# Low parts of all split weight tiles subtracted on VectorE, none on GpSimd

## The chip, the cores and the metric

The kernel runs on one core of one Trainium2 chip. The metric is the device time of one execution in microseconds (us). PE is TensorE, DVE is VectorE, ACT is ScalarE, POOL is GpSimd, SP the engine from whose queue the weights are loaded. Times inside the program are counted from the start of the profiled span.

## The reference

Two stacked blocks on 256 tokens of width 1024, all in float32. The first mixes a gated delta rule (8 heads) with a dilated window attention and ends in a mixture of 64 experts; the second prepends 16 meta tokens and runs an attention layer and a short-convolution layer, each followed by a squared-ReLU layer. Cut to what matters here:

```python
def first_block(x, c, w_ada, ..., w_in, ...):
    cs = jax.nn.silu(c)
    mod = (cs @ w_ada[l] + b_ada[l])[:, None, :]
    h = _rms(x, g_mix[l]) * (1.0 + sc1) + sh1
    proj = h @ w_in[l]                       # 1024 x 11280
    y_a = gated_deltanet(gq, gk, gv, gz, gb, ga, ...)
    y_b = dilated_mixture(dil_q, dil_k, dil_v, ...)
    merged = sigmoid(gate_a) * (y_a @ w_up_gdn[l]) + sigmoid(gate_b) * (y_b @ w_up_dil[l])
    x = x + gt1 * (merged @ w_out[l])
    x = x + gt2 * moe_ffn(h2, ...)

def second_block(x, meta_tokens, norm_g, w_in, w_out, ..., w_up, w_down):
    for i in range(2):
        h = _rmsnorm(hres, norm_g[i, 0])
        m = _diff_attention(h, ...) if i == 0 else _short_conv(h, ...)
        hres = hres + _rmsnorm(m, norm_g[i, 1])
        h = _rmsnorm(hres, norm_g[i, 2])
        hres = hres + _rmsnorm(_sqrelu_mlp(h, w_up[i], w_down[i]), norm_g[i, 3])
```

## The kernel before

Every dense product outside the experts is made of three products of float32r tiles, so that nearly all bits of float32 are kept: weights and activations are each split into a high part and a low part, and `mm3` (L168 to L175) adds high by high (L172), high by low (L173) and low by high (L175). A weight tile of 1024 x 256 comes from HBM through a ring of four buffers (`load`). `split` (L148 to L159) makes the two parts of half of it, 128 partitions by 1024 numbers: ACT copies the high part `hi` (L154), then one engine subtracts it from the weights to get the low part `lo` (L158). That engine is POOL for some of the tiles and DVE for the rest. The tiles `hi` and `lo` rotate through three buffers each in the first stage and through four in the second block. PE needs `hi` first and `lo` for the last third of the product.

Two counters choose the engine. `pool_every = 4` holds while the delta rule, the dilated attention and the gates are computed (from 42 to 452 us, called the delta-rule stage below): there every fourth split goes to POOL, 21 in all. `pool_next = 2` is set ahead of four layers of the second block (attention, first squared-ReLU layer, convolution, second squared-ReLU layer) and sends the next two splits to POOL, 8 in all. One small tile more (`gbl`, L563) is subtracted on POOL once. Besides, POOL computes all powers of -1/2 (`rpow` L236, `token_factors` L1533, L667) and some small scalings.

A scheduling layer sets the order of the instructions on each engine from its own estimates, within the data's order. Each engine then works through its own list in that order; an instruction that waits holds back what stands behind it on its engine.

The end of a layer in the second block is one chain. `mix_out` (L1677 to L1694) makes the last eight products `m` on short tiles (256 numbers), adds their squares into `accm` (ACT squares `sq`, DVE adds at L1516), and `add_normed` then sums over the partitions on PE (L1529), reduces (`tp`, L1531), takes the power on POOL (`tr`, L1533), spreads it on PE (L1540), and updates the residual on DVE (L1587, L1588), from which ACT and DVE make the next layer's activations `hsh` and `hsl`. Three groups of ten matmuls that fill time (`warm`, L1572) stand between. The next layer begins with `wide` (L208), three tiles side by side. The second squared-ReLU layer follows `mix_out` in the same way with 256 tokens for 258. The end of the first squared-ReLU layer, ahead of the convolution, has the same chain behind a plain product.

Of the kernel before, what the change touches and what calls it, by code (L numbers as in the profile page):

```python
# [10 lines left out]
F32 = mybir.dt.float32  # L11
# [3 lines left out]
ALU = mybir.AluOpType  # L15
# [107 lines left out]
class Kern:  # L123
    def __init__(self, ctx, tc, a, out, dbg=None, stop=None):
        self.ctx, self.tc, self.nc, self.a, self.out = ctx, tc, tc.nc, a, out
        self.dbg = dbg or {}
        self.stop = stop
        self.ns, self.pool_every, self.pool_next = 0, 0, 0
        self.steps, self.queued = [], []
        E = ctx.enter_context  # L130
        self.cst = E(tc.tile_pool(name="cst", bufs=1))
        self.ring = E(tc.tile_pool(name="ring", bufs=4))
# [15 lines left out]
    def split(self, v, hp, shape=None):  # L148

        nc = self.nc  # L150
        a, b = v.shape[1], v.shape[2]
        hi = hp.tile([128, 1024], F32R, tag="hi", name="hi")[:, :a * b].rearrange("p (a b) -> p a b", a=a)
        lo = hp.tile([128, 1024], F32R, tag="lo", name="lo")[:, :a * b].rearrange("p (a b) -> p a b", a=a)
        nc.scalar.activation(hi, v, AF.Copy)  # L154
        self.ns += 1
        eng = nc.gpsimd if self.pool_next > 0 or self.pool_every and self.ns % self.pool_every == 0 else nc.vector
        self.pool_next -= 1
        eng.tensor_tensor(lo, v, hi.bitcast(F32), op=ALU.subtract)  # L158
        return hi, lo  # L159

    def wcols(self, w, col, n=256):
# [193 lines left out]
    def phase_a(self):  # L355
        nc, tc, a, cst = self.nc, self.tc, self.a, self.cst
        with ExitStack() as st:
# [31 lines left out]
            with tc.manual_schedule():  # L389
# [55 lines left out]
                v = self.load(self.wcols(w_in, OFF_GK), (8, 256))  # L445
# [13 lines left out]
            with tc.tile_pool(name="wka", bufs=1) as wk:  # L459
                self.second_setup(xt.tile([16, D], F32, name="mt", tag="thb"),  # L460
                                  wk.tile([128, 4, 64], F32, name="lv", tag="cv", bufs=2),
                                  wk.tile([128, 2, 64], F32, name="lvp", tag="cth", bufs=2),
                                  pm.tile([128, 512], F32, tag="m", name="ps_mt"))
                late = (y for c in (2, 4, 3, 5) for u in range(2) for y in self.ada(c, u))
                self.pool_every = 4
                self.fill = lambda: next(late, None)
                dil = [self.dil_pair(n, w_in, x, hp, wk) for n in range(2)]
                for pr in range(4):
                    t = self.gdn_proj(pr, w_in, x, hp, wk)
                    if pr == 0:  # L470
                        nc.sync.dma_start(self.CA, a["consts"][:, C_LVL:C_ND])
                        to_channels(x_tok, xT)
                    self.gdn_pair(pr, t, wk)
                    for n in (0, 0, 0, 0, 1)[pr:pr + 1] if pr < 2 else ((0, 0), (1,))[pr - 2]:
                        next(dil[n])
                list(dil[1])
                th = (xt.tile([128, 8, T], F32, name="tha", tag="xnT"), xt.tile([128, 8, T], F32, name="thb", tag="thb"))
                for u in range(4):
                    for n, off in enumerate((OFF_GA, OFF_GBT)):
                        def sink_g(ft, ps, n=n, u=u):  # L480
                            nc.scalar.activation(th[n][:, u * 2 + ft, :], ps, AF.Tanh, scale=0.5)
                        self.dense(self.wcols(w_in, off + u * 256), x, T, sink_g, hp, pp)
                        self.fill()
                list(late)
            self.dump("yaT", ya)
            self.dump("ybT", yb)
            self.pool_every = 0
            sh.close()
            self.before_b()
            hp = sh.enter_context(tc.tile_pool(name="hpf", bufs=3, side="right"))  # L490
# [65 lines left out]
    def gdn_scalars(self, w_in, x, hp, wk):  # L556

        nc, a, cst, pm = self.nc, self.a, self.cst, self.pm
        small = self.small
        v = self.load(w_in[:, OFF_GB:OFF_GB + 16].rearrange("(j p) c -> p j c", p=128), (8, 16))  # L560
        hi, lo = (wk.tile([128, 8, 16], F32R, tag=t, name=n) for t, n in (("dv0", "gbh"), ("dv1", "gbl")))
        nc.scalar.activation(hi, v, AF.Copy)
        nc.gpsimd.tensor_tensor(lo, v, hi.bitcast(F32), op=ALU.subtract)  # L563
        xh, xl = x
        gb = cst.tile([128, 2, 16], F32, name="gb")
        ps = pm.tile([128, 512], F32, tag="m", name="ps_gb")
        self.mm3(ps[:16, :T], lambda j: hi[:, j, :], lambda j: lo[:, j, :], lambda j: xh[:, j, :], lambda j: xl[:, j, :], 8)
        gbt = wk.tile([16, T], F32, name="gbt", tag="cv", bufs=2)
        nc.vector.tensor_copy(gbt, ps[:16, :T])
        ps = pm.tile([128, 512], F32, tag="m", name="ps_gbt")  # L570
        for t in range(2):
            nc.tensor.transpose(ps[:, t * 16:t * 16 + 16], gbt[:, t * 128:t * 128 + 128], self.ident[:16, :16])
        nc.vector.tensor_copy(gb, ps[:, :32].rearrange("p (t c) -> p t c", t=2))
        self.beta = cst.tile([128, 2, 8], F32, name="beta")
        nc.scalar.activation(self.beta, gb[:, :, 0:8], AF.Tanh, scale=0.5)
        nc.vector.tensor_scalar(self.beta, self.beta, 0.5, 0.5, op0=ALU.mult, op1=ALU.add)
        al = cst.tile([128, 2, 8], F32, name="alog")
        nc.scalar.dma_start(al[:, 0, :], pbc(a["gdn_a_log"][0]))
        nc.scalar.dma_start(al[:, 1, :], pbc(a["gdn_dt_bias"][0]))
        nc.scalar.activation(al[:, 0, :], al[:, 0, :], AF.Exp)  # L580
        z = small.tile([128, 2, 8], F32, tag="z", name="z")
        for t in range(2):
            nc.vector.tensor_tensor(z[:, t, :], gb[:, t, 8:16], al[:, 1, :], op=ALU.add)

        u = small.tile([128, 2, 8], F32, tag="u", name="u")
        nc.vector.scalar_tensor_tensor(u, z, -1.0, z, op0=ALU.mult, op1=ALU.min)
        nc.scalar.activation(u, u, AF.Exp)
        s = small.tile([128, 2, 8], F32, tag="s", name="s")
        nc.vector.tensor_scalar(s, u, 2.0, None, op0=ALU.add)
        nc.vector.reciprocal(s, s)  # L590
        nc.vector.tensor_tensor(s, s, u, op=ALU.mult)
        s2 = small.tile([128, 2, 8], F32, tag="s2", name="s2")
        nc.vector.tensor_tensor(s2, s, s, op=ALU.mult)
        q = small.tile([128, 2, 8], F32, tag="q", name="q")
        nc.vector.tensor_scalar(q, s2, 2.0 / 17, None, op0=ALU.mult)
        for k in (15, 13, 11, 9, 7, 5, 3):
            nc.vector.scalar_tensor_tensor(q, q, 2.0 / k, s2, op0=ALU.add, op1=ALU.mult)
        nc.vector.scalar_tensor_tensor(q, q, 2.0, s, op0=ALU.add, op1=ALU.mult)
        nc.vector.scalar_tensor_tensor(q, z, 0.0, q, op0=ALU.max, op1=ALU.add)
        self.g = cst.tile([128, 2, 8], F32, name="g")  # L600
        for t in range(2):
            nc.vector.scalar_tensor_tensor(self.g[:, t, :], q[:, t, :], -1.0, al[:, 0, :], op0=ALU.mult, op1=ALU.mult)

        ps = pm.tile([128, 512], F32, tag="m", name="ps_gc")
        gf = self.g.rearrange("p a b -> p (a b)")
        nc.tensor.matmul(ps[:, 0:16], self.ut, gf, start=True, stop=True)
        nc.tensor.matmul(ps[:, 16:24], self.lt, self.g[:, 0, :], start=True, stop=True)
        self.ngc = cst.tile([128, 3, 8], F32, name="ngc")
        nc.vector.tensor_scalar(self.ngc[:, 0:2, :].rearrange("p a b -> p (a b)"), ps[:, 0:16], -1.0, None, op0=ALU.mult)
        nc.vector.tensor_copy(self.ngc[:, 2, :], ps[:, 16:24])  # L610
        self.dump("beta", self.beta)
        self.dump("g", self.g)
# [978 lines left out]
    def phase_c(self):  # L1591
        nc, tc, a, cst = self.nc, self.tc, self.a, self.cst
        with ExitStack() as st:
# [7 lines left out]
            with tc.tile_pool(name="ppa", bufs=3, space=PSUM) as self.pp, \  # L1601
# [5 lines left out]
                b = None  # L1607
                bank = lambda: self.pt.tile([128, 512], F32, tag="t", name="ps_row")
                oT = xp.tile([128, 8, 258], F32R, name="oh", tag="oh"), xp.tile([128, 8, 258], F32R, name="ol", tag="ol")
                self.pool_next = 2  # L1610
                qkv, b = self.diff_proj(0, h, lambda: self.token_factors(acc, 272, bank), ap, hp,
                                        lambda r: self.kept(self.rows_of(*r, 272, bank), 272, sp))
                for pr in range(4):
# [12 lines left out]
            h, acc = self.gained(4, 258, xp, self.upd)  # L1626
            yT = xp.tile([128, 8, 258], F32R, name="oh", tag="oh"), xp.tile([128, 8, 258], F32R, name="ol", tag="ol")
            w = a["w_in_2"][1]
            self.pool_next = 2
            with tc.tile_pool(name="cvp", bufs=2) as ap:  # L1630
                for u in range(4):
                    c2, y = [None] * 2, [None] * 2
# [64 lines left out]
    def mlp(self, layer, n, hp, sp, xp, bank):  # L1697
# [1 line left out]

        nc, a, pp = self.nc, self.a, self.pp  # L1700
        h, acc0 = self.gained(layer * 4 + 2, n, xp, self.upd)
        self.pool_next = 2
        m = None if layer else xp.tile([128, 8, 258], F32, name="m", tag="m")
        wu, wd = a["w_up_2"][layer], a["w_down_2"][layer]
        acc, add = self.token_sums(sp, n, "q")
# [344 lines left out]
```

## Time and profile before

| what | value |
|---|---|
| median of 3 runs | 1692.33 us (1687.98 to 1697.52) |
| the profiled execution's own time | 1685.4 us |
| its span, first to last instruction | 1683.3 us |
| granted TensorE clock, mean over the span | 0.983 |
| PE / DVE / ACT / POOL busy | 95% / 57% / 40% / 8% |

A clock share of 1.00 is 2.4 GHz, 0.50 is 1.2 GHz. The busy share of PE is one of modelled ends of pipelined matmuls, so small waits do not show in it. In the views, "idle before" and the name in brackets tell what an engine waited for; `x8` at a row's end counts merged instructions, and their time is that from the first one's start to the last one's end. The durations of neighbours on one engine overlap a little, so that a step in the list costs somewhat less than its duration.

### The profile page before, as it was taken

The numbers are of one execution on the slowest core, as the hardware profiler recorded it, in microseconds if no ns is written. First come the engines' busy times: TensorE is split into PE (matmuls) and PEld (weight loads), VectorE is DVE, ScalarE is ACT, GpSimd is POOL, SyncE is SP. The second block draws the span as 40 slices with busy tenths as digits, with TensorE's granted clock in tenths as the row PEclk, the third lists the DMA queues.
The fourth block names the chain that finished last, engine by engine and source line by source line (L and its number), as shares of the span: only waits on it lengthen the run. The fifth ranks groups of instructions, "written<-read, shape, count | busy, mean of one in ns | idle before, by whom it ended". The sixth has DMA issues, their size and how long they took to land. (4 is left out here: it accounts for less than half of the span.)

```text
span 1683.3 us, 31624 instructions
## 1 busy us (share of the span) xinstructions
PE 1604.9 (95%) x12847; PEld 1406.0 (84%) x12847; DVE 960.0 (57%) x2069; ACT 676.1 (40%) x1353; POOL 135.9 (8%) x120
## 2 busy tenths in 40 slices
PE   6999999999999999998999997998999999989998
PEld 3899999999997667655766656888999999989998
DVE  5879796975475223322332345666765457686644
ACT  4534335344453212211221214555554345465532
POOL 0211212132100000000000001012000010010000
PEclk8999999999999999999999998999999999989999
DMA  9534442456389799999999995322555545455552
GB/s 315 200 127 150 136 140 91 161 182 189 123 275 381 303 420 418 420 418 419 420 368 409 419 412 166 109 88 88 176 176 183 190 154 165 148 161 184 183 177 75
DMA packets 198496, 392.04 MB, mean 233 GB/s; under 512 B 8760, under 2 KB 158780, under 8 KB 173260
## 3 DMA queue, kind: packets, MB, share of 16 engines
q1 hardware_dynamic: 197916, 389.76, 63.7%
q8 instruction: 102, 1.67, 0.4%
q14 instruction: 46, 0.38, 0.1%
q10 hardware_dynamic: 432, 0.23, 0.1%
HBM read 388.92 MB, written 1.05 MB: 232 GB/s over the span
## 5 line engine op out<-in xcount | busy, mean ns | idle before, releaser
L154 ACT ACTIVATE hi<-w 128x1024 fp32r<-128x1024 f32 (+3 forms) x316 | 314.8, 1003 | 345.2 <-PE proj L173 231.2
L158 DVE TENSOR_TENSOR lo<-w,hi 128x1024 fp32r<-128x1024 f32 (+3 forms) x287 | 330.6, 1156 | 175.1 <-ACT hi L154 164.7
L1327 PE MATMUL ps_gu<-w,X 128*64 128x256 f32 (+2 forms) x2112 | 218.7, 384 | 7.3 <-DMA w<-in_w_exp_up 6.6
L1327 PEld LDWEIGHTS ps_gu<-w,X 128*64 128x64 f32 (+2 forms) x2112 | 143.9, 133 | 84.7 <-issue 14.9
L172 PE MATMUL proj<-hsh,hi 128*128 128x258 f32 (+2 forms) x824 | 208.3, 288 | 0.0
L173 PE MATMUL proj<-hsl,hi 128*128 128x258 f32 (+2 forms) x824 | 205.9, 285 | 0.0
L172 PE MATMUL proj<-hh,hi 128*128 128x256 f32 x640 | 167.1, 294 | 0.4 <-DVE cv L621 0.2
L173 PE MATMUL proj<-hl,hi 128*128 128x256 f32 x640 | 164.8, 291 | 0.1
L172 PEld LDWEIGHTS proj<-hsh,hi 128*128 128x128 f32 x824 | 156.7, 190 | 1.8 <-issue 1.1
L173 PEld LDWEIGHTS proj<-hsl,hi 128*128 128x128 f32 x824 | 157.5, 191 | 0.1
L158 POOL TENSOR_TENSOR lo<-w,hi 128x1024 fp32r<-128x1024 f32 x29 | 70.0, 2416 | 925.9 <-ACT hi L154 875.7
L172 PEld LDWEIGHTS proj<-hh,hi 128*128 128x128 f32 x640 | 122.9, 192 | 1.8 <-DVE cv L621 0.4
L173 PEld LDWEIGHTS proj<-hl,hi 128*128 128x128 f32 x640 | 122.5, 191 | 0.8 <-DVE hl L427 0.3
L1335 DVE SCALAR_TENSOR_TENSOR tg<-tg,ps_gu 128x256 f32<-128x256 f32 x30 | 12.6, 421 | 181.4 <-ACT tg L1334 181.4
L175 PE MATMUL proj<-hsh,lo 128*128 128x258 f32 (+2 forms) x824 | 115.7, 282 | 0.0
L1365 PE MATMUL ps_d<-w,hT 128*64 128x512 f32 (+2 forms) x528 | 109.9, 597 | 0.5 <-DVE hT L1351 0.5
L175 PEld LDWEIGHTS proj<-hsh,lo 128*128 128x128 f32 x824 | 106.3, 188 | 0.0
L175 PE MATMUL proj<-hh,lo 128*128 128x256 f32 x640 | 101.7, 291 | 0.0
L1334 ACT ACTIVATE tg<-ps_gu 128x256 f32<-128x256 f32 x30 | 11.5, 385 | 213.7 <-PE ps_gu L1327 213.7
L172 PE MATMUL proj<-oh,hi 128*128 128x258 f32 (+1 forms) x384 | 96.1, 285 | 0.4 <-ACT oh L1983 0.4
L173 PE MATMUL proj<-ol,hi 128*128 128x258 f32 (+1 forms) x384 | 95.1, 283 | 0.0
L1365 PEld LDWEIGHTS ps_d<-w,hT 128*64 128x64 f32 (+2 forms) x528 | 33.9, 131 | 64.9 <-issue 43.8
(488 smaller groups left out, 3210.0 us busy)
## 6 DMA issues: line engine op xcount, KB each, us to landing
w<-in_w_in SPq DMA_DIRECT2D x66, 1024.0 KB, 5.2
w<-in_w_exp_up SPq DMA_DIRECT2D x64, 1024.0 KB, 16.1
w<-in_w_exp_gate SPq DMA_DIRECT2D x64, 1024.0 KB, 16.3
w<-in_w_exp_down SPq DMA_DIRECT2D x64, 1024.0 KB, 19.8
w<-in_w_up SPq DMA_DIRECT2D x32, 1024.0 KB, 5.5
w<-in_w_down SPq DMA_DIRECT2D x32, 1024.0 KB, 5.2
w<-in_w_ada SPq DMA_DIRECT2D x24, 1024.0 KB, 5.5
w<-in_w_out SPq DMA_DIRECT2D x8, 768.0 KB, 4.4
```

The source lines that it names most:

```text
L154: nc.scalar.activation(hi, v, AF.Copy)
L158: eng.tensor_tensor(lo, v, hi.bitcast(F32), op=ALU.subtract)
L172: nc.tensor.matmul(ps, wh(j), xh(j), start=(first and j == 0), stop=False)
L173: nc.tensor.matmul(ps, wh(j), xl(j), start=False, stop=False)
L175: self.last_mm = nc.tensor.matmul(ps, wl(j), xh(j), start=False, stop=(last and j == n - 1))
L1327: nc.tensor.matmul(ps[b0:b1, c * 256:c * 256 + 256], Q.X[:, j, n * 128 + b0:n * 128 + b1], w[:, j, :], start=(j == 0), stop=(j == KC - 1))
L1334: nc.scalar.activation(tg, ps[:, 0:256], AF.Tanh, scale=0.5)
L1335: nc.vector.scalar_tensor_tensor(tg, tg, 1.0, ps[:, 0:256], op0=ALU.add, op1=ALU.mult)
L1365: nc.tensor.matmul(psd[hf][b0:b1, :], hT[:, f, b0:b1], v[i][:, f, halves[hf]], start=(f == 0), stop=(f == 1))
```

## The change

All subtractions of `split`, and the small one of `gbl`, are put on DVE; the two counters and the lines that set them go. POOL keeps the powers, the small scalings, one memset and one small product. Nothing else in the source differs, but the scheduling layer, given other engines, writes other lists.

```diff
-        self.ns, self.pool_every, self.pool_next = 0, 0, 0
...
         nc.scalar.activation(hi, v, AF.Copy)
-        self.ns += 1
-        eng = nc.gpsimd if self.pool_next > 0 or self.pool_every and self.ns % self.pool_every == 0 else nc.vector
-        self.pool_next -= 1
-        eng.tensor_tensor(lo, v, hi.bitcast(F32), op=ALU.subtract)
+        nc.vector.tensor_tensor(lo, v, hi.bitcast(F32), op=ALU.subtract)
         return hi, lo
...
-                self.pool_every = 4
...
-            self.pool_every = 0
...
         nc.scalar.activation(hi, v, AF.Copy)
-        nc.gpsimd.tensor_tensor(lo, v, hi.bitcast(F32), op=ALU.subtract)
+        nc.vector.tensor_tensor(lo, v, hi.bitcast(F32), op=ALU.subtract)
...
-                self.pool_next = 2
...
-            self.pool_next = 2
...
-        self.pool_next = 2
```

The list of DVE at the end of the attention layer, before the change. `accm` is the running sum of squares, `m` one of the last products, `lo` a low part (256 numbers: the last short tile of `mix_out`; 1024: the next layer's), `tp` the reduction ahead of the power.

```order
L1516 SCALAR_TENSOR_TENSOR accm<-accm,sq 128x258
L1692 TENSOR_TENSOR m<-m,proj 128x258
L1516 SCALAR_TENSOR_TENSOR accm<-accm,sq 128x258
L158 TENSOR_TENSOR lo<-w,hi 128x256
L1516 SCALAR_TENSOR_TENSOR accm<-accm,sq 128x258
L1692 TENSOR_TENSOR m<-m,proj 128x258
L1516 SCALAR_TENSOR_TENSOR accm<-accm,sq 128x258
L158 TENSOR_TENSOR lo<-w,hi 128x1024
L1531 TENSOR_REDUCE tp<-ps_row 128x3
L158 TENSOR_TENSOR lo<-w,hi 128x1024
```

The same place after the change (lines are numbered 4 to 8 lower from here on).

```order
L1510 SCALAR_TENSOR_TENSOR accm<-accm,sq 128x258
L1684 TENSOR_TENSOR m<-m,proj 128x258
L1510 SCALAR_TENSOR_TENSOR accm<-accm,sq 128x258
L154 TENSOR_TENSOR lo<-w,hi 128x256
L1510 SCALAR_TENSOR_TENSOR accm<-accm,sq 128x258
L154 TENSOR_TENSOR lo<-w,hi 128x1024
L1510 SCALAR_TENSOR_TENSOR accm<-accm,sq 128x258
L1684 TENSOR_TENSOR m<-m,proj 128x258
L154 TENSOR_TENSOR lo<-w,hi 128x1024
L1525 TENSOR_REDUCE tp<-ps_row 128x3
L154 TENSOR_TENSOR lo<-w,hi 128x1024
```

Two long low parts now stand ahead of `tp` where one stood, the first of them between two sums and ahead of the last `m`; the layer's fourth low part, which stood behind `tp`, has gone behind the residual's update. The second squared-ReLU layer's beginning has the same new list.

The list of ACT at the same place, before: `hi` is a high part, `sq` a square, `accm` the last square.

```order
L1514 ACTIVATE sq<-m 128x258 x3
L154 ACTIVATE hi<-w 128x1024
L1514 ACTIVATE sq<-m 128x258
L154 ACTIVATE hi<-w 128x1024
L1511 ACTIVATE accm<-m 128x258
L154 ACTIVATE hi<-w 128x1024
```

And after:

```order
L1508 ACTIVATE sq<-m 128x258 x3
L153 ACTIVATE hi<-w 128x1024
L1508 ACTIVATE sq<-m 128x258
L153 ACTIVATE hi<-w 128x1024 x2
L1505 ACTIVATE accm<-m 128x258
```

The last high part has moved ahead of the last square.

The list of DVE in the delta-rule stage, third pair of heads, inside the inversion of the 64 x 64 triangles (`X`, `Y` are its iterates, `acc` a running sum of the modulation's products), before:

```order
L741 TENSOR_TENSOR X<-consts,Y 128x128
L742 TENSOR_TENSOR X<-consts,ps_p_2551 128x128
L326 SCALAR_TENSOR_TENSOR acc<-w,cs,acc 128x512
L726 SCALAR_TENSOR_TENSOR Y<-ps_p_2558,bk,consta 128x128 x4
L326 SCALAR_TENSOR_TENSOR acc<-w,cs,acc 128x512
L746 TENSOR_TENSOR X<-X,ps_p_2569 128x256 x2
```

And after:

```order
L735 TENSOR_TENSOR X<-consts,Y 128x128
L736 TENSOR_TENSOR X<-consts,ps_p_2551 128x128
L154 TENSOR_TENSOR lo<-w,hi 128x1024
L720 SCALAR_TENSOR_TENSOR Y<-ps_p_2558,bk,consta 128x128 x4
L154 TENSOR_TENSOR lo<-w,hi 128x1024
L740 TENSOR_TENSOR X<-X,ps_p_2569 128x256 x2
```

Low parts stand between the iterates where sums of the modulation stood; the sums have moved to later places.

## Rows read from the trace of the kernel before

**Rows 1.** The page, part 1: busy time, share of span, instructions.

```profile
PE 1604.9 (95%) x12847; PEld 1406.0 (84%) x12847; DVE 960.0 (57%) x2069; ACT 676.1 (40%) x1353; POOL 135.9 (8%) x120
```

**Rows 2.** The page, part 5: the low parts on DVE and on POOL.

```profile
L158 DVE TENSOR_TENSOR lo<-w,hi 128x1024 fp32r<-128x1024 f32 (+3 forms) x287 | 330.6, 1156 | 175.1 <-ACT hi L154 164.7
...
L158 POOL TENSOR_TENSOR lo<-w,hi 128x1024 fp32r<-128x1024 f32 x29 | 70.0, 2416 | 925.9 <-ACT hi L154 875.7
```

**Rows 3.** Timeline of POOL, DVE and PE, end of attention: start, duration, instruction.

```profile
1172.17 4.86 POOL L158 TENSOR_TENSOR lo<-w,hi 128x1024 fp32r<-128x1024 f32 x2 [7.44 <-ACT hi L154]
...
1172.43 2.38 DVE L1516 SCALAR_TENSOR_TENSOR accm<-accm,sq 128x258 f32<-128x258 f32 x1
1174.74 0.41 DVE L1692 TENSOR_TENSOR m<-m,proj 128x258 f32<-128x258 f32 x1
1175.08 2.24 DVE L1516 SCALAR_TENSOR_TENSOR accm<-accm,sq 128x258 f32<-128x258 f32 x1
1177.23 0.41 DVE L158 TENSOR_TENSOR lo<-w,hi 128x256 fp32r<-128x256 f32 x1
...
1179.22 1.22 DVE L158 TENSOR_TENSOR lo<-w,hi 128x1024 fp32r<-128x1024 f32 x1
...
1177.70 0.80 PE L175 MATMUL proj<-oh,lo 128*128 128x258 f32 x2 [4.60 <-DVE lo L158]
```

**Rows 4.** The same timeline at the end of the convolution layer.

```profile
1476.65 2.44 DVE L1516 SCALAR_TENSOR_TENSOR accm<-accm,sq 128x256 f32<-128x256 f32 x1
...
1481.97 0.79 PE L175 MATMUL proj<-oh,lo 128*128 128x256 f32 x2 [4.68 <-DVE lo L158]
```

**Rows 5.** Windows: length, PE, PEld, DVE, ACT, POOL busy, clock, DMA.

```profile
1178.00:1180.00 2.00, 2.00 (x10) 2.00 (x10) 1.46 (x3) 1.00 (x2) 0.00 (x0) 0.50 0.40 97
...
1186.00:1188.00 2.00, 1.66 (x14) 1.45 (x13) 1.59 (x5) 0.34 (x1) 0.00 (x0) 0.98 0.95 307
...
1376.00:1378.00 2.00, 2.00 (x21) 2.00 (x19) 1.50 (x2) 0.51 (x2) 0.00 (x0) 1.00 0.65 221
```

**Rows 6.** Chain that ended last, three layer ends: start, share in us, work.

```profile
1178.50 2.13 PE ps_row L1572 x10
...
1188.22 3.89 PE proj L208 x30
...
1375.90 1.19 PE ps_row L1572 x10
...
1382.18 4.27 PE proj L208 x33
...
1482.76 2.13 PE ps_row L1572 x10
...
1491.56 3.96 PE proj L208 x33
```

**Rows 7.** Window of the whole delta-rule stage, columns as in the windows above.

```profile
42.00:452.00 410.00, 398.06 (x3255) 386.31 (x3254) 311.66 (x704) 175.76 (x353) 87.80 (x74) 1.00 0.46 147
```

**Rows 8.** Timeline of POOL and DVE in the delta-rule stage.

```profile
230.65 2.35 POOL L158 TENSOR_TENSOR lo<-w,hi 128x1024 fp32r<-128x1024 f32 x1 [7.88 <-PE proj L172]
...
230.69 2.46 DVE L741 TENSOR_TENSOR X<-consts,Y 128x128 f32<-128x128 f32 x1
233.07 0.27 DVE L742 TENSOR_TENSOR X<-consts,ps_p 128x128 f32<-128x128 f32 x1
```

**Rows 9.** Waits of PE, 40 to 455 us: total, times, longest.

```profile
PE ps_p L724 <- DVE X L741: 1.5, 1, 1.5
...
PE ps_p L724 <- DVE X L746: 0.7, 1, 0.7
```

**Rows 10.** Waits of DVE in the same stretch.

```profile
DVE lo L158 <- ACT hi L154: 27.2, 16, 4.5
```

**Rows 11.** Timeline of POOL: two of the same powers.

```profile
1378.60 0.85 POOL L1533 TENSOR_TENSOR tr<-tp,mhalf 128x3 f32<-128x3 f32 x1 [5.82 <-DVE tp L1531]
...
1394.51 1.77 POOL L1533 TENSOR_TENSOR tr<-tp,mhalf 128x3 f32<-128x3 f32 x1 [15.06 <-DVE tp L1531]
```

## The prediction

> **What bounds the kernel now.** I read the busy shares first [rows 1]: PE is busy for 95% of the span, so an instruction moved between DVE and POOL matters only where PE stands still for it. The groups then show the two prices of a low part [rows 2]: 2.42 us on POOL, 1.16 us on DVE (a mean over long and short tiles; a long one alone takes 1.22 us [rows 3]). POOL has the time: it is busy 8%. The question is what else a low part on POOL costs, so I went to the timelines of the two engines side by side.
>
> At the end of the attention layer POOL runs two low parts from 1172.17 to 1177.03 us, and just then two DVE sums of 258 numbers take 2.38 and 2.24 us [rows 3]. Their neighbour `m`, as wide, takes 0.41 us in the middle of the second POOL instruction. The sums read two tiles in SBUF; `m` reads one there and one in PSUM. So POOL's instruction does not slow DVE in general: it holds a DVE instruction with two SBUF inputs until it is done. The short `lo` stands behind the second sum in DVE's list, and PE waits 4.60 us for it. The convolution layer's end repeats this, with 4.68 us [rows 4].
>
> The windows show a second loss there [rows 5]. After the wait PE runs at a granted clock of 0.50, the 1.2 GHz level, until about 1186 us. At the end of the first squared-ReLU layer, which has the same chain and no such wait, the clock stays at 1.00. The chain gives the price [rows 6]: from the first filling matmul to the next layer's first product it is 1188.22 - 1178.50 = 9.72 us at the end of attention, 1491.56 - 1482.76 = 8.80 us after the convolution, and 1382.18 - 1375.90 = 6.28 us at the undisturbed one.
>
> The delta-rule stage is the third place. There 21 low parts run on POOL, and one that started just ahead of it makes an `X` of 128 numbers take 2.46 us [rows 8]; `m` above took 0.41 us for twice the width. PE has independent projections to run meanwhile, so most such blocks never reach it: of the waits of PE in this stage [rows 9], six are for a delta-rule result of DVE, 1.5 us the longest and 0.7 us the shortest, 6.9 us together. One more, for a POOL power, stands between them and isn't counted. Five of the six follow right behind a POOL low part, the first being that of [rows 8].
>
> **The change, part by part.**
>
> *End of attention.* From the first blocked sum to the short `lo` it is now 1177.23 - 1172.43 = 4.80 us for a sum, `m` and a sum. At 0.41 us each, the length of the unblocked one, it is 1.23 us. PE's last product then starts 3.6 us earlier, and PE stands still for about 1 us instead of 4.60. With so short a wait I expect the clock to stay at 1.00, and the rest of the chain to take 6.28 instead of 9.72 us: 3.4 us more. Against this the new list puts two long low parts on DVE ahead of `tp`, where one stood. The first delays the last `m` by 1.2 us, and the last square on ACT now stands behind one more high part. Their cover is the ten filling matmuls, 1.19 us at full clock [rows 6], and the twelve sums on PE. One low part just fits; what sticks out is the second, with ACT's delay, and I take 1.0 us, near one low part's price. Uncovered, it would be 2.4 us; covered, nothing. The sum is -3.6 - 3.4 + 1.0 = -6.0 us. The layer's fourth low part goes behind the residual's update; PE needs it only when the 72 matmuls of the three tiles side by side and 16 more are through, so it costs nothing, and 1.2 us if that cover fails.
>
> *End of the convolution.* The same steps: 3.6 us for the block [rows 4], 8.80 - 6.28 = 2.5 us for the clock, 1.0 us back: -5.1 us.
>
> *The other two pairs.* Two low parts ahead of the attention layer run while PE and DVE wait for sums of the new activations; two ahead of the convolution run inside a product that PE paces. No PE wait is tied to either, and on DVE they displace nothing on the chain: 0, with 1.2 us a pair if the cover is gone. `gbl`: 0.
>
> *Delta-rule stage.* The six waits go: -6.9 us at best. In return DVE has 21 more instructions of about 1.2 us, 25 us, in a stage where it is busy for 311.66 of 410 us, 76% [rows 7]; it also loses the blocked time, which is of the same size, so its load hardly grows. But the low parts now stand in its list ahead of iterates. One in this place holds back the iterate behind it, and if its high part is late, for longer: low parts already wait 27.2 us for ACT in this stage [rows 10]. What one costs PE I bound by 0 and by its 1.2 us. Six of 21 blocks of up to 2 us reached PE; I let the same share, with half a low part's length, 0.6 us, and about as much again for lists that have changed everywhere, come back: 6 x 0.6 = 3.4 to 3.6 us. I take 3.4, so -3.5 us here. SP's loads wait for the low parts to release the ring's buffers, so they move with them; PE waits for no weights in this stage, the view of [rows 9] has no DMA.
>
> A power on POOL takes 0.85 us alone and 1.77 us when a long low part on DVE has just begun [rows 11]: 0.9 us each. Such meetings exist already at both layer ends, where a low part follows `tp` in both lists, and the few new ones are inside the 3.4 us. The Trainium skill, "SBUF — State Buffer", section "Who interferes with whom", says that the two engines share a read and write port as an exclusive lock, and that the second to issue is blocked until the first is done. This agrees with both sides of it here, the 2.38 us sum and the 1.77 us power.
>
> *Sum.* -6.0 - 5.1 - 3.5 = -14.6 us. The profiled execution took 1685.4 us, 0.4% under the median of the runs shown; it would take 1670.8. Against the median of 1692.33 it is 1677.7 us, 0.9% faster. Nothing downstream takes it back: the experts' loads are issued when the first stage releases its buffers, so they start earlier by what that stage gains.
>
> **The rivals.** Within 0.5% (8.5 us) is about what a measurement of this kernel can't tell from no change.
>
> *The clock falls all the same* (chance 0.15). PE still waits for the short `lo`, the last square and the power, some 1 us each. If the chip answers to these together as it does to one wait of 4.6 us, only the blocks are gained: 2 x (3.6 - 1.0) + 3.5 = 8.7 us, 1683.6 us. Against it: the undisturbed end has its waits too and stays at 1.00 [rows 5].
>
> *DVE becomes the limit of the delta-rule stage, and the kernel is slower* (chance 0.08). If each of the 21 low parts held PE for its whole 1.2 us, 25 us would be lost, and 6.9 + 11.1 gained: +7 us, 1699.5 us. It ends slower once each costs PE over 18.0/21 = 0.86 us. For it: DVE is busy 76% there, low parts stand between iterates now, and each has to wait for ACT in order. Against it: blocks of twice that length reached PE in only six cases. The Trainium skill, "Perfetto Trace Analysis", section "Optimizing Scalar/DVE Operations", says that moving work off a saturated DVE, even to GpSimd, may make sense, and warns that the shared port may undo it. The first half speaks against this change; the 6.9 us of waits behind POOL bear out the second.
>
> *The layer ends gain, the stage gives most of it back* (chance 0.15): the new lists cost PE 9.7 us in the stage where 6.9 go, +2.8 us, and both low parts stick out at each end, 2.4 us for 1.0. Then -11.1 + 2.8 + 2 x 1.4 = -5.5 us, 1686.8 us, no change that can be told.
>
> *My forecast* has 0.62; its own range is 1672 to 1683 us, from the full gain of the stage and nothing back at the ends (-13.1 - 6.9 = -20.0) to a stage that gains nothing (-9.7 with one more low part sticking out). The whole range reaches to the clock's and the give-back rivals: 1665 to 1689 us; the low end adds some 5 us by which the runs shown differ around their median. Faster: the forecast and two thirds of the clock's rival, 0.72; same 0.20; slower 0.08.
>
> **What would show it.** In the new profile the two sums must take 0.4 us and PE's wait for the short `lo` must be 1 us or less at both ends; the windows behind must show a clock of 1.00; from the first filling matmul to the next first product it must be 6.3 to 7.5 us. PE's waits for delta-rule results must sum to under 6.9 us, and the layer ends must lie earlier by 3.5 us (end of the stage) and by 14.6 us (end of the span). I am wrong if the clock still falls, if waits for `accm` or `tp` replace the ones removed, or if the stage ends no earlier than at 452 us.

## The result, and the profile after

The changed kernel took 1664.64 us, the median of four runs from 1664.39 to 1665.74; the kernel before took 1691.03 beside it. The ratio is 0.984, with an interval of 0.981 to 0.987: 26.4 us less, where 14.6 were forecast. That is under the forecast's own range of 1672 to 1683 us and 0.4 us under its whole range of 1665 to 1689. Measured again (below, the changed kernel once more) it took 1668.29 us, 24.0 us less. The profiled execution took 1664.41 us (span 1662.4), against 1685.4: 21.0 us less.

The page of the changed kernel, its parts 1 and 5, shows the move, as [rows 1, 2] for before:

```profile
PE 1596.5 (96%) x12847; PEld 1400.3 (84%) x12847; DVE 960.2 (58%) x2099; ACT 675.6 (41%) x1353; POOL 66.3 (4%) x90
...
L154 DVE TENSOR_TENSOR lo<-w,hi 128x1024 fp32r<-128x1024 f32 (+3 forms) x316 | 362.6, 1153 | 169.9 <-ACT hi L153 159.3
```

DVE carries 29 low parts and `gbl` more, and its busy time is what it was, 960.2 for 960.0 us: the time in which its instructions stood held (33.6 us, counted below) was about as long as the new work, 29 low parts of 1.2 us.

The end of the attention layer, in the timelines of DVE, PE, POOL and ACT (start, duration, instruction), answers to [rows 3]:

```profile
1163.11 0.42 DVE L1510 SCALAR_TENSOR_TENSOR accm<-accm,sq 128x258 f32<-128x258 f32 x1
1163.44 0.42 DVE L154 TENSOR_TENSOR lo<-w,hi 128x256 fp32r<-128x256 f32 x1
...
1165.92 1.22 DVE L154 TENSOR_TENSOR lo<-w,hi 128x1024 fp32r<-128x1024 f32 x1
...
1167.47 1.22 DVE L154 TENSOR_TENSOR lo<-w,hi 128x1024 fp32r<-128x1024 f32 x1
...
1163.92 0.51 PE L171 MATMUL proj<-oh,lo 128*128 128x258 f32 x2 [0.82 <-DVE lo L154]
...
1169.46 1.22 PE L1534 MATMUL ps_row<-consts,tr 128*128 128x128 f32 x6 [0.81 <-POOL tr L1527]
...
1167.63 1.77 POOL L1527 TENSOR_TENSOR tr<-tp,mhalf 128x3 f32<-128x3 f32 x1 [12.91 <-DVE tp L1525]
...
1164.17 1.99 ACT L153 ACTIVATE hi<-w 128x1024 fp32r<-128x1024 f32 x2
1166.07 0.40 ACT L1505 ACTIVATE accm<-m 128x258 f32<-128x258 f32 x1
```

The sum takes 0.42 us where it took 2.38, and PE waits 0.82 us for the short `lo`, not 4.60. But the last square (`accm` on ACT) stands behind two high parts, and the power `tr` takes 1.77 us beside a low part on DVE, so PE waits for it. The windows behind it, columns as in [rows 5], show what follows:

```profile
1168.00:1170.00 2.00, 1.19 (x9) 0.99 (x8) 0.69 (x1) 0.00 (x0) 1.40 (x1) 0.93 0.96 303
1170.00:1172.00 2.00, 2.00 (x12) 2.00 (x11) 1.29 (x4) 0.04 (x1) 0.00 (x0) 0.50 0.93 317
1172.00:1174.00 2.00, 2.00 (x14) 2.00 (x14) 2.00 (x6) 2.00 (x6) 0.00 (x0) 0.71 0.06 17
1174.00:1176.00 2.00, 2.00 (x19) 2.00 (x18) 2.00 (x7) 1.07 (x3) 0.00 (x0) 1.00 0.00 0
```

The clock falls once more to 0.50, its 1.2 GHz level, for (0.07 + 0.50 + 0.29) x 2 x 2 = 3.4 us in all, and is back before 1174 us. (Each window's shortfall from 1.00, times its 2 us, is doubled, since a shortfall of 0.50 is the whole window at 0.50.) The chain then has the filling matmuls and the next layer's first product at these times, for the ends of attention and of convolution [rows 6]:

```profile
1170.67 2.34 PE ps_row L1566 x10
1173.02 4.08 PE proj L204 x33
...
1468.24 2.09 PE ps_row L1566 x10
1470.81 3.87 PE proj L204 x33
```

So the product behind attention starts 15.2 us earlier (1188.22 to 1173.02), and that behind the convolution 20.75 us (1491.56 to 1470.81). At 441.5 us the delta-rule stage is where it was at 452. Its window [rows 7], and PE's waits in it [rows 9], are now:

```profile
42.00:441.50 399.50, 394.63 (x3255) 384.48 (x3254) 311.49 (x727) 176.46 (x355) 37.81 (x52) 1.00 0.47 154
...
PE ps_kb L820 <- POOL rk L232: 1.5, 1, 1.5
...
PE ps_d L676 <- DVE g L596: 0.9, 1, 0.9
```

The same 3255 matmuls take 10.5 us less. PE's idle time falls from 410 - 398.06 = 11.9 to 399.5 - 394.63 = 4.9 us, by 7.1; the other 3.4 us are in PE's busy time, so in the pace of its matmuls. No wait for X, Y, Q or A is left; of those for a delta-rule result of DVE one is, 0.9 us for `g`.

### The profile page after: what moved, and what is told of

The parts are those of the page before. It is cut to its first block, busy times and chain, and to the rows that moved or that the text cites. A ratio compares the mean times of both kernels' runs of the same rounds, so it can differ in the third digit from the quotient of the medians.

```text
span 1662.4 us, 31607 instructions
## 1 busy us (share of the span) xinstructions
PE 1596.5 (96%) x12847; PEld 1400.3 (84%) x12847; DVE 960.2 (58%) x2099; ACT 675.6 (41%) x1353; POOL 66.3 (4%) x90
## 5 line engine op out<-in xcount | busy, mean ns | idle before, releaser
L154 DVE TENSOR_TENSOR lo<-w,hi 128x1024 fp32r<-128x1024 f32 (+3 forms) x316 | 362.6, 1153 | 169.9 <-ACT hi L153 159.3
L1328 ACT ACTIVATE tg<-ps_gu 128x256 f32<-128x256 f32 x30 | 11.5, 385 | 213.8 <-PE ps_gu L1321 213.8
L171 PEld LDWEIGHTS proj<-hh,lo 128*128 128x128 f32 x640 | 85.5, 191 | 0.1
```

What stands on the lines that cost most here:

```text
L154: nc.vector.tensor_tensor(lo, v, hi.bitcast(F32), op=ALU.subtract)
L171: self.last_mm = nc.tensor.matmul(ps, wl(j), xh(j), start=False, stop=(last and j == n - 1))
L1328: nc.scalar.activation(tg, ps[:, 0:256], AF.Tanh, scale=0.5)
```

## Experiments

Each gain below is against the kernel before on the same chip. "Held" is worked out from the trace: over all DVE instructions that lie beside a low part (or the instruction put in its place) on POOL, what they took beyond the 30th percentile of the same instruction and shape, each counted once; 33.6 us in the kernel before. The last two columns are of the profiled execution: the time at a clock of 0.50 inside the delta-rule stage, by the trace's own record of the clock, and the stage's length (from the first matmul into `ps_mt` to the first into `ps_shc`) less half of that time. In the first two profiles they are 3.4 and 413.0 us before, 0 and 404.3 us after the change.

| kernel | us, median (from, to) | ratio, interval | gain, us | held, us | at 0.50 in the stage, us | stage less half of that, us |
|---|---|---|---|---|---|---|
| stage alone changed | 1675.28 (1675.02, 1681.2) | 0.9902, 0.9882 to 0.9922 | 16.6 | 7.6 | 13.7 | 403.4 |
| layer ends alone | 1684.46 (1679.3, 1686.05) | 0.9951, 0.9932 to 0.9969 | 7.4 | 25.5 | 17.1 | 413.3 |
| every eighth on POOL | 1677.49 (1676.84, 1679.69) | 0.9916, 0.99 to 0.9933 | 14.8 | 14.1 | 10.2 | 409.7 |
| shadow, two inputs | 1704.06 (1700.84, 1707.78) | 1.0072, 1.0054 to 1.009 | -12.2 | 41.1 | 27.3 | 420.3 |
| shadow, one input | 1678.62 (1675.37, 1680.8) | 0.9931, 0.9914 to 0.9947 | 11.5 | 12.9 | 6.8 | 409.0 |
| shadow, writes only | 1675.96 (1671.88, 1679.06) | 0.9914, 0.9897 to 0.9932 | 14.2 | under 0.5 | 13.7 | 406.5 |
| low parts doubled on DVE | 1683.18 (1679.85, 1686.28) | 0.9947, 0.9929 to 0.9965 | 8.7 | 0 | 17.1 | 410.0 |
| 21 low parts left out | 1667.12 (1665.07, 1667.48) | 0.9859, 0.984 to 0.9878 | 23.0 | 0 | 3.4 | 403.1 |
| ends, two behind the power | 1668.03 (1665.4, 1670.71) | 0.9871, 0.9853 to 0.9889 | 22.1 | 0 | 3.4 | 403.9 |
| ends, one behind the power | 1666.68 (1661.0, 1669.51) | 0.9835, 0.9816 to 0.9854 | 25.6 | 0 | 17.1 | 403.5 |
| changed kernel once more | 1668.29 (1664.2, 1672.5) | 0.9852, 0.983 to 0.9873 | 24.0 | 0 | 10.2 | 403.6 |
| kernel before once more | 1691.86 (1687.87, 1697.27) | 0.9998, 0.9984 to 1.0011 | 0.4 | 33.2 | 6.8 | 413.7 |

**Which part gives what.** The stage alone: in the kernel before

```diff
-                self.pool_every = 4
+                self.pool_every = 0
```

and `gbl` on `nc.vector`.

> The change in the delta-rule stage alone: its 21 low parts and gbl go to VectorE, the four pairs at the layer ends stay on GpSimd. By the prediction's terms it gives 3.5 us, 6.9 of waits less 3.4 that come back, and the two long sums at the layer ends (2.4 us each) stay. If GpSimd's instructions hold VectorE and nothing comes back, the stage ends about 10 us earlier, as in the changed kernel, and the time is about 10 us under the profiled execution of the kernel before. If the scatter of the kernel before (1688 to 1697 us) comes from meetings of the two engines in this stage, the five times lie within 2 us of each other; if it comes from the layer ends, they scatter as before.

The layer ends alone:

```diff
-                self.pool_next = 2
+                self.pool_next = 0
```

at all its places.

> The change at the four pairs behind the layer ends alone; the stage keeps every fourth low part on GpSimd. By the prediction's terms 11.1 us less (6.0 and 5.1), about 10.6 us by the two traces. The sums ahead of the norm take 0.42 us, and TensorE waits under 1 us for the short low part. The time scatters as before if the stage makes the scatter. Together with the stage's run the gains should add up to the whole one of 21 us between profiles; if they don't, the two parts are not independent.

The two gains, 16.6 and 7.4 us, add up to the 24.0 of the whole change as measured again, though each median holds its own share of the clock's falls. The stage is worth far more than 3.5 us: with the time at 0.50 taken out, it is 9.6 us shorter (413.0 to 403.4). The rest of the 16.6 us goes with the clock, whose mean is 0.985 at this kernel's median and 0.980 at that of the kernel before. The scatter follows neither part alone: three runs of the stage's kernel lie within 0.3 us, the profiled one 6 us above, with 13.7 us at 0.50 in its stage.

**How many low parts it takes.** The changed kernel, with every eighth low part of the stage on `nc.gpsimd`.

> The changed kernel with every eighth low part of the delta-rule stage on GpSimd (9 or 10, where the kernel before has 21), and none elsewhere. If each held instruction costs alike, the loss is near half of that of 21, between the changed kernel (1664.6) and the one with the layer ends alone changed (1684.5): 1672 to 1676 us. If only a few blocks reach TensorE, those that fall just ahead of a delta-rule iterate, it depends on which are left: 1664 to 1684 us, and each loss shows as a wait for X, Y, Q or A.

PE's waits in the stage show delta-rule results again:

```profile
PE ps_kk L696 <- DVE A L700: 2.4, 2, 1.8
...
PE ps_p L723 <- DVE X L740: 1.1, 1, 1.1
...
PE ps_p L735 <- DVE Y L725: 0.5, 1, 0.5
```

Against the changed kernel's second measurement it loses 9.2 us, just over half of the stage's 16.6, with ten of the 21 low parts on POOL. Between the two profiles, which have the same 10.2 us at 0.50 in the stage, the stage differs by 6.1 us (409.7 and 403.6), of some 10 us for all 21. That is about a price for each, but the waits above, 4.0 us, also bear out the other case, a few places that reach PE; this run doesn't tell the two apart.

**What holds DVE.** At the places where POOL made the low part, the changed kernel gets one more POOL instruction on data that nobody reads; DVE still makes the low part.

```diff
         nc.vector.tensor_tensor(lo, v, hi.bitcast(F32), op=ALU.subtract)
...
+            nc.gpsimd.tensor_tensor(jk, v, hi.bitcast(F32), op=ALU.subtract)
```

> The changed kernel, and at the 29 places where GpSimd made the low part before it makes the same subtraction once more into a tile that nobody reads (2-byte output, one instruction). VectorE still makes the low part that TensorE waits for. If it is GpSimd's two-input instruction that holds VectorE, the loss comes back without any change to who needs what: instructions of VectorE with two SBUF inputs take 2 us beside it, and the time is near that of the kernel before, 1680 to 1695 us, or above since VectorE now carries the low part too. If the new order of the lists, or TensorE's waiting for GpSimd's slower low part, made the gain, the time stays within 3 us of 1664.6.

With one input the added line is `nc.gpsimd.tensor_scalar(jk, hi.bitcast(F32), 2.0, 1.0, ...)`.

> As the shadow run with two inputs, but GpSimd's extra instruction reads one tile (the high part, times a constant plus a constant, into the same unread tile). If any long GpSimd instruction over 1024 numbers holds VectorE's two-input instructions, the loss is near that of the two-input shadow, 39 us over the changed kernel. If only an instruction with two SBUF inputs holds them, the time stays within 4 us of 1664.6 and no VectorE instruction beside it takes longer than alone.

For writes alone it is the same on 8 numbers a partition, and then two `nc.gpsimd.memset(jk, ...)`.

> As before, but GpSimd reads only 8 numbers a partition, to be started by the same high part, and then writes the unread tile twice with a constant: a load on GpSimd that reads nothing. If GpSimd's being busy, or its writes, hold VectorE, some tens of us are lost; if only reads with two inputs do, the time stays within 4 us of 1664.6.

The same stretch of the stage in the timelines of POOL and DVE, with two inputs, with one, and with writes only:

```profile
423.06 2.52 POOL L159 TENSOR_TENSOR junk<-w,hi 128x1024 bf16<-128x1024 f32 x1 [9.14 <-ACT hi L154]
...
423.28 2.52 DVE L880 TENSOR_SCALAR S<-S,rd 128x384 f32<-128x384 f32 x1
```

```profile
403.16 1.19 POOL L159 TENSOR_SCALAR junk<-hi 128x1024 bf16<-128x1024 f32 x1 [9.16 <-ACT hi L154]
...
403.36 1.20 DVE L880 TENSOR_SCALAR S<-S,rd 128x384 f32<-128x384 f32 x1
```

```profile
404.71 0.37 POOL L159 TENSOR_SCALAR junk<-hi 128x8 bf16<-128x8 f32 x1 [9.16 <-ACT hi L154]
405.14 1.07 POOL L160 MEMSET junk<- 128x1024 bf16 x1
...
404.90 0.42 DVE L882 TENSOR_SCALAR S<-S,rd 128x384 f32<-128x384 f32 x1
405.23 1.22 DVE L155 TENSOR_TENSOR lo<-w,hi 128x1024 fp32r<-128x1024 f32 x1
```

`S` takes 2.52, 1.20 and 0.42 us. Beside a POOL instruction that reads 1024 numbers it ends 0.2 us after it; beside the memset, a POOL instruction that only writes, the low part takes the 1.22 us that it takes alone. The loss comes back under the shadow though nobody waits for POOL's result, so the rival by which PE waited for a slow POOL falls, and so does the order of the lists as the sole cause. Not all of the shadow's loss is held time: PE also waits 4.8 us for POOL's powers there (3.2 us with one input), 1.5 us in the changed kernel. The expectation that one input or writes cost nothing was wrong. One input holds DVE too, for less time. And writes only, with 2.41 us of POOL work a place and nothing held, still lose some 10 us against the changed kernel measured again, in part in another way: POOL's powers stand behind them in its list. PE's waits and the window of that kernel's stage:

```profile
PE ps_kb L831 <- POOL rk L240: 4.8, 3, 2.3
```

```profile
42.00:451.50 409.50, 400.97 (x3263) 390.82 (x3262) 311.55 (x727) 177.09 (x356) 87.41 (x115) 0.98 0.47 150
```

The wait grows by 3.3 us. The clock of 0.98 stands for 13.7 us at 0.50, which cost half of that. Since the changed kernel itself had 10.2 us of it in its second profile, only the wait can be put down to the memsets: without the clock's part the stage is 406.5 us, 2 to 3 us over the changed kernel's. In the kernel before, the wait for `rk` was 1.5 us, as after, so the longest wait for a power was no part of this change's gain.

**What a low part costs DVE.** Doubled: the shadow's added line, on `nc.vector`.

> The changed kernel, and at the same 29 places VectorE makes the low part twice (the second into a tile that nobody reads), so its load grows by 29 x 1.2 = 35 us, 25 of it in the delta-rule stage. If a low part there costs TensorE next to nothing, since projections cover it, the stage ends within 4 us of the changed kernel's, and the layer ends lose at most 1.2 us for each copy that stands ahead of the norm: 1665 to 1673 us. If VectorE is near its limit in the stage (the rival by which a low part costs TensorE its whole 1.2 us), 1690 us or more; by the prediction's 3.4 us for 21 low parts, some 5 us.

Left out, every fourth of the stage:

```diff
+        if self.skip_every and self.ns % self.skip_every == 0:
+            return hi, hi
         nc.vector.tensor_tensor(lo, v, hi.bitcast(F32), op=ALU.subtract)
```

> The changed kernel without every fourth low part of the delta-rule stage: no engine makes it, and its product takes the high part in its place, so these products are wrong and the rest is the same work for TensorE. It prices the 21 low parts that VectorE took over. If they cost TensorE nothing, as the vanished waits say, the time stays within 2 us of 1664.6. If VectorE's load counts throughout (the doubled low parts cost 18.5 us for 29), the stage ends up to 15 us earlier, 1650 us. By the prediction's term, 3.4 us earlier, 1661 us.

The windows of the stage, doubled and left out:

```profile
42.00:457.00 415.00, 404.24 (x3264) 394.03 (x3265) 333.92 (x747) 177.14 (x356) 40.30 (x52) 0.98 0.47 148
```

```profile
42.00:442.00 400.00, 396.36 (x3255) 385.92 (x3254) 289.05 (x706) 176.57 (x355) 37.31 (x52) 1.00 0.48 153
```

With 22 us less on DVE the stage is no shorter: 400.0 us for 399.5, and without the clock's part it is 403.1 us for 403.6 and 404.3. With 22 us more it takes some 15 us longer, about 0.7 us for each of the 21, but 17.1 us at 0.50 are in this, where the first profile of the changed kernel has none. Without the clock's part it is 410.0 us, some 6 us longer: 0.3 us for each. Whether the doubled low parts made any of the falls isn't shown. So DVE had room for the 21 low parts once nothing was held, and each more would cost PE 0.3 to 0.7 us.

**The scatter.** The two kernels once more, unchanged.

> The changed kernel once more, unchanged. If the even times of its first four runs (1664.4 to 1665.7 us) belong to the kernel, all runs lie within 2 us. If they were a run of luck, since the clock's short falls in the delta-rule stage come and go from one execution to the next with the same lists (the kernel without the 21 low parts and the one with other layer ends show one of 3.41 us each), some runs lie 1.5 to 6 us higher at a mean clock of 0.985 to 0.987.

> The kernel before once more, for a second profile. If its scatter is the clock's, the profile shows the same waits and the same held instructions as the first (38 us more than alone, in all) and differs from it in the time at 0.50 in the delta-rule stage, half of which accounts for the difference in time within 1 us. If the scatter is of the blocks (other meetings of the two engines), the held time and the waits of TensorE differ by about the difference in time.

A window of the kernel before, first profile, then two windows of the changed kernel, first profile and second:

```profile
189.00:197.00 8.00, 7.83 (x51) 7.34 (x51) 3.61 (x10) 3.84 (x9) 4.11 (x7) 0.79 0.00 0
```

```profile
64.00:72.00 8.00, 8.00 (x69) 7.82 (x68) 6.28 (x14) 4.06 (x9) 2.49 (x4) 1.00 0.04 7
...
346.00:354.00 8.00, 8.00 (x67) 7.82 (x66) 7.04 (x14) 2.77 (x6) 1.83 (x2) 1.00 0.48 156
```

```profile
64.00:72.00 8.00, 8.00 (x43) 8.00 (x44) 3.94 (x12) 2.57 (x6) 2.45 (x4) 0.57 0.01 2
...
346.00:354.00 8.00, 7.50 (x47) 7.07 (x48) 4.29 (x9) 2.75 (x7) 3.64 (x6) 0.79 0.55 194
```

In the second profile of the changed kernel PE does 43 matmuls where it did 69. A clock of 0.57 and 0.79 over 8 us each is 6.9 and 3.4 us at 0.50; half of the 10.3 is 5.1 us, and the second profile's stage ends 5.0 us later, with the same waits of PE to 0.1 us. So these falls come and go in one and the same program, and the first four even times were luck. Five profiles of the changed kernel's stage (the kernel twice, the stage alone and the two other orders of the ends) confirm the price: with 0, 3.4, 10.2, 13.7 and 17.1 us at 0.50 the stage less half of that is 403.4 to 404.3 us. For the kernel before the second profile agrees only in part: held time (33.2 us) and waits are the same, the stage has 3.4 us more at 0.50, which makes 1.7, and is 2.7 us longer, but the whole execution is 4.3 us longer and the rest isn't settled. Over 17 runs of the kernel before, the time goes from 1687.91 us at a mean clock of 0.983 to 1697.22 at 0.976; the changed kernel's five from 1664.2 at 0.988 to 1672.5 at 0.982. At the same mean clock, 0.982, a run of the kernel before took 1689.97 us, 17.5 us more.

**The layer ends.** In the changed kernel, the low parts two to four behind `tr`, the high parts three and four behind the last square (`nw` counts the next product's splits, `mh` and `ml` are a split's instructions for the high and the low part):

```diff
+        if 3 <= self.nw <= 4:
+            self.after(mh, self.last_sq)
+        if 2 <= self.nw <= 4:
+            self.tc.add_manual_dep(ml.ins, self.last_tr.ins.name, ...)
```

> The changed kernel, and at the ends of the attention and the convolution layer the low parts two to four of the next product stand behind the power on GpSimd, and the high parts three and four behind the last square on ScalarE; nothing else in the lists differs. In the changed kernel the last square stands behind two high parts (1.99 us) and the power takes 1.77 us beside a low part. If these two are what is left at the ends, each end's chain gets 2 us shorter, 3.4 with the clock at 1.00 throughout, so 4 to 7 us less, 1658 to 1661 us. If the low parts that now come later hold up the next product, nothing or a loss up to 3 us.

The two low parts then ran together ahead of the residual's update, the gain at either end was under 0.5 us, and no gain shows in the times. Then the same with `if 3 <= self.nw <= 4` for the low parts too:

> The run before held two low parts behind the power, and both then stood ahead of the residual's update, 2.36 us. Here only the third low part waits for the power and the high parts three and four for the last square; VectorE's list is that of the changed kernel. If the power's 1.77 us and the square's wait of 2 us are what is left, the chain from the first filling matmul to the next first product gets 1.5 to 2.5 us shorter at either end (8.55 and 8.47 us in the changed kernel), and the time 3 to 5 us. If VectorE's update is the limit again, under 1 us.

POOL, ACT and a window at the end of attention:

```profile
1175.83 0.85 POOL L1535 TENSOR_TENSOR tr<-tp,mhalf 128x3 f32<-128x3 f32 x1 [12.89 <-DVE tp L1533]
...
1174.25 0.42 ACT L1513 ACTIVATE accm<-m 128x258 f32<-128x258 f32 x1 [1.77 <-DVE m L1692]
...
1178.00:1180.00 2.00, 1.20 (x10) 1.00 (x9) 2.00 (x6) 0.90 (x3) 0.00 (x0) 1.00 1.02 351
```

The first filling matmuls and the next product in PE's timeline at the two ends, in the changed kernel:

```profile
1164.26 1.34 PE L1566 MATMUL ps_row<-oh 128*128 128x256 f32 x10
...
1172.81 0.42 PE L204 MATMUL proj<-hsh,hi 128*128 128x258 f32 x1
...
1462.09 1.36 PE L1566 MATMUL ps_row<-oh 128*128 128x256 f32 x10
...
1470.56 0.60 PE L204 MATMUL proj<-hsh,hi 128*128 128x256 f32 x3
```

And with one low part behind the power:

```profile
1172.47 1.35 PE L1574 MATMUL ps_row<-oh 128*128 128x256 f32 x10
...
1179.66 0.51 PE L212 MATMUL proj<-hsh,hi 128*128 128x258 f32 x2 [0.80 <-ACT hsh L1560]
...
1468.95 1.34 PE L1574 MATMUL ps_row<-oh 128*128 128x256 f32 x10
...
1475.81 0.38 PE L212 MATMUL proj<-hsh,hi 128*128 128x256 f32 x1
```

The power takes 0.85 us, the clock stays at 1.00, and from the first filling matmul to the next product it is 7.2 and 6.9 us, not 8.6 and 8.5: 3.0 us in both. Not all of it is the order's, for the clock's falls come and go here too: it stayed at 1.00 at attention's end in the run with every eighth low part on POOL (7.9 us) and at the convolution's in the changed kernel's second profile (7.5 us). Against these the order gives 0.7 and 0.6 us. The runs overlap (1661.0 to 1669.51 us against 1664.2 to 1672.5), so that it beats the changed kernel is shown by the trace's ends alone, in one profile, and not by the times.

## Why the forecast was too small

*The mechanism was right:* a POOL low part holds DVE instructions until it is done, and taking it away shortens both layer ends and the stage. That the layer ends would carry three quarters of it was wrong.

*End of attention and of convolution, -6.0 and -5.1 us.* Between the two profiles they gave 5.0 and 5.4 us, near the 11.1 forecast (15.2 less the 10.2 by which the expert layers already ended earlier; 20.75 less the 15.4 at the layer's start, 1382.18 to 1366.80); alone, 7.4 us together in the median. The blocks were sized right: PE's wait for the short `lo` fell by 3.8 us at attention. The clock term was not: the clock did fall, which the prediction names as a sign of being wrong, for a shorter time, and the chain behind the wait gave the other 1.2 us, where 3.4 - 1.0 was forecast. The rival in which the clock falls all the same was half right. The cause that it names, the waits for the square and the power, is what the run with one low part behind the power removed, and the clock stayed up. But it also stayed up once at either end with the changed kernel's order, so that cause isn't shown.

*Delta-rule stage, -6.9 + 3.4 us: the step that failed.* Of the waits 0.9 us are left for 6.9 (PE's idle time fell by 7.1 us). The 3.4 us that I let come back did not: without the 21 low parts altogether the stage is at most 1.2 us shorter (403.1 for 403.6 and 404.3 us). The 3.4 had no firm source: six times 0.6 are 3.6, and the "as much again" for changed lists isn't in the sum. And a loss was not in the sum: the clock at 0.50 inside this stage. The kernel before had one such stretch (its window from 189 to 197 us has a clock of 0.79, 3.4 us), the changed one none, 1.7 us; the other 1.7 of the busy time are not settled. That is 10.5 us between profiles. The 1.7 us were chance: between the second two profiles the stage differs by 8.2 us, with 6.8 us at 0.50 before and 10.2 after. Without the clock's part it is 8.7 and 10.1 us, where 3.5 was forecast. So nearly all that the waits gave was kept, and 1.6 to 2.7 us came on top from PE's busy time, whose cause stays open.

*The rest of the median's gain.* I took the profiled gain over to the median. Between profiles the gain was 21.0 us, and 21.4 in the second pair (1689.68 to 1668.29), but 26.4 and 24.0 between medians. The profiled execution of the kernel before was its fastest, and the first four runs of the changed kernel were lucky: the mean clock is 0.980 at the median of the kernel before, 0.984 in the changed kernel measured again and 0.988 in the first four runs. Time at half the clock costs half of itself, so (0.988 - 0.980) x 1690 = 13.5 us is the most that this can explain in the first comparison, 6.8 us in the second. Up to 6.8 us of either lie at the two layer ends, where 10.2 us at 0.50 became 3.4 or less, and stand in the terms above. That the removed waits make the falls inside the stage rarer is not shown: with the old stage the profiles have 3.4, 6.8 and 17.1 us of them (the layer ends alone being the third), with the new one 0, 3.4, 10.2, 13.7 and 17.1. Measured again, at 1668.29 us, the kernel lies inside the whole range of 1665 to 1689, so that the first median fell below it was luck; that both lie under the forecast's own range was not, and comes mainly from the stage.

*DVE as the limit* didn't come to pass. A second copy of the same low parts costs 0.7 us each in its profile and 0.3 without the clock's part, where the rival wins from 0.86. The Trainium skill's lock ("SBUF — State Buffer", section "Who interferes with whom") agrees with the sums held for 2.38 and 2.24 us. The Trainium skill, in the same section, says that a DVE instruction with two SBUF inputs contends with a GpSimd instruction that reads SBUF and not with one that only writes. The trace agrees: beside the memset the low part took 1.22 us, as alone.

## What to carry to other kernels

A slow engine with free time is no free place: price an instruction there by what it holds on its neighbour, instruction by instruction, and by what stands behind it in its own list. Total busy time that stays the same after a move is a sign that the new work filled time in which the old had been held. Before a few us are claimed or doubted, profile the same kernel twice: here the same program differed by 5 us in one stage, through the clock alone. With half of the time at 0.50 taken off, five profiles of that stage agreed within 0.9 us.

## What was not expected of the hardware

A POOL instruction with one SBUF input holds DVE as well (`S` 1.20 us for 0.42), and `S`, a DVE instruction with one SBUF tile and a number per partition as inputs, is held like one with two tiles. A reduction of one SBUF tile was not: in the kernel before `nm` took 0.94 us at 272.33 us, in the middle of a POOL low part, and 0.944 us is the mean of its four. POOL writes of 0.95 us hold nothing. The granted clock fell to 0.50 for 6.9 and 3.4 us in one execution and not in another of the same program, whose list of waits of PE is the same.
